# Second block of a two-block model: third sum read from PSUM, more products issued ahead with their results put aside, operands combined in place, another tail

## The chip, the core and the metric

The kernel runs on one core of one Trainium2 chip. The metric is device time in microseconds (us) of one execution. The kernel before was run three times: 2788.42 us in the median, 2787.32 to 2789.34. The engines of the core are called as the profile calls them: PE (matrix multiplications), PEld (its weight loads), DVE (vector), ACT (scalar), POOL (GpSimd), SP (the queue that issues almost all transfers of this part).

## The reference, cut to what matters

Two blocks are computed on a sequence of 1024 rows by 1024 features, in float32. Only the second one is touched here, of which only the last layer's end matters: a gated short convolution and a feed-forward part.

```
h = modulate(rmsnorm(x, norm1_g), sh1, sc1)          # 1024 x 1024
y = short_conv_mixer(h, conv_w_in, conv_w, conv_w_out)   # h @ (1024 x 3072), a gate and a
                                                     # 3-tap convolution, then @ (1024 x 1024)
x = x + g1 * y
h = modulate(rmsnorm(x, norm2_g), sh2, sc2)
gate, up = split(h @ ffn_w_in)                       # D_FF = 2816 columns each
x = x + g2 * ((silu(gate) * up) @ ffn_w_out)
return rmsnorm(x, final_g)
```

## The kernel before, in words

Each of the four big products is done in 2 x 2 blocks with seven block products instead of eight (P1 to P7, a Winograd scheme). Every float32 operand is split in a high and a low part, `split` (L106 the ACT cast that makes the high part, L107 the DVE subtraction that makes the low part), and each block product is three matmuls (high by high, high by low, low by high) for each of four blocks of 128 of the contraction: 12 matmuls of 128 x 512.

The stretch has four stages.

- **Conv, first product.** 12 sets (8 pairs of feature blocks, 4 gates), one set of 84 matmuls each. A set takes its left operands from the weights (`left_operands`: two loads of 512 KB through a ring of four raw buffers, then four sums on DVE, L1212 to L1216, and splits) and its right operands from the activations. These are seven slots in the pages H and HB, made by `right_operands` (four DVE operations L1177 to L1180 and `split_slots` L1167/L1169) for each of four blocks t of 128 rows. P1 and P2 need only right operands of the first 512 rows (B21, B11), all the others also some of the last 512 rows.
- **Conv, second product.** `out_products` (matmul L1335) runs over seven names in the order P1, P6, P2, P7, P5, P4, P3; `use` is called for each name and t with the result. `conv_use` closes the layer: the uses of P4 and P3 call `third`, which normalizes a row block, transposes it on PE (L1374) and makes the right operands of the feed-forward part.
- **Feed-forward, first product.** 22 sets as in the conv stage, `tail` L1241 to L1258 in each.
- **Feed-forward, second product.** `out_products` with `ffn_use`, whose P4 and P3 uses end with the final normalization (`fourth`, L1534) and the stores (L1535).

In a set, `head` does P1 and copies its result to an E tile (L1238). `tail` then does P6 (L1246 adds P1's copy), P5 (ACT copies the result from PSUM, L1248; POOL adds the sum so far, L1249: this is the third sum), P7 (L1251, DVE adds the third sum to the result), P2 (onto P1 in PSUM), P3 (L1255) and P4 (L1257). A set has four PSUM banks, and sets alternate between banks 0 to 3 and 4 to 7; P4 is accumulated onto P7's bank, so its first matmul comes after L1251. `ahead` L1260 does P1 and P2 of the first two sets of a stage before their other products.

Beside the sets POOL makes the second product's operands: `spill` combines what two sets gave (L1274 to L1280), and `sums_steps` combines blocks of the second weight (L1291 to L1307, their loads L1289 to L1306); both store to HBM. These steps are dealt out by `mix`, some at each tick.

The order on each engine is not that of the code: a scheduler sets it when the kernel is built, from the dependences and its own times of the instructions. SP and POOL are queues in that order as well.

Of the kernel before, what the change touches and what calls it, by code (L numbers as in the profile page):

```python
# [8 lines left out]
F32R = mybir.dt.float32r  # L9
AF = mybir.ActivationFunctionType  # L10
# [17 lines left out]
def program(tc, I, out):  # L28
# [4 lines left out]
    with ctx:  # L33
# [939 lines left out]
        def out_steps(half, i):  # L973
# [3 lines left out]
            def start():  # L977
                st["r"] = rr1()
# [139 lines left out]
        if 0:  # L1118
            with tc.manual_schedule(engines={mybir.EngineType.PE}):
                attention()  # L1120
        else:
            attention()
        for n in range(len((40, 43, 48, 52, 56, 59, 63)), 8):
            for x in out_steps(1, n):
                x()
# [9 lines left out]
        HBt = Split(sb(P3, "HB", 8192, F32R))  # L1135
        PA = Split(sb(P3, "PA", 2048, F32R))
        RAW.append(sb(P3, "raw3", 1024))
        E = sb(P3, "E", 18 * 512)
# [33 lines left out]
        def right_operands(where, t, h1, h2, tmp):  # L1172

            b11, b21, b12, b22 = h1[:, 0:512], h1[:, 512:1024], h2[:, 0:512], h2[:, 512:1024]
            t1, t2, t3, t4 = (tmp[:, i * 512:(i + 1) * 512] for i in range(4))
# [5 lines left out]
            split_slots(("T1", "T2"), where, t, tmp[:, 0:1024])  # L1181
            split_slots(("T3", "T4"), where, t, tmp[:, 1024:2048])


        n_set = {"i": 0}

        def left_operands(w, c1, c2):
# [3 lines left out]
            r1, r2 = next_raw(), next_raw()  # L1191
            SY.dma_start(r1.rearrange("p (k n) -> p k n", k=8), rows(w, c1, 128))
            SY.dma_start(r2.rearrange("p (k n) -> p k n", k=8), rows(w, c2, 128))
# [3 lines left out]
            def page():  # L1197
                w = wpages[turn["w"] % len(wpages)]
                turn["w"] += 1
                return w  # L1200
            g1, g2, g3 = page(), page(), page()
# [4 lines left out]
            def first():  # L1206
                split(g1.r[:, 0:1024], g1.r[:, 1024:2048], g1.f[:, 0:1024], r1)

            def rest():
                split(pa[:, 0:512], pa[:, 512:1024], paf[:, 0:512], r2[:, 0:512])  # L1210
# [3 lines left out]
                split(g2.r[:, 0:1024], g2.r[:, 1024:2048], g2.f[:, 0:1024], r2)  # L1214
                V.tensor_tensor(a12, a21, a12, ALU.subtract)
                V.tensor_tensor(a11, a11, a12, ALU.subtract)  # L1216
                split(g3.r[:, 0:1024], g3.r[:, 1024:2048], g3.f[:, 0:1024], r1)
            return dict(first=first, rest=rest, bank=4 * (i % 2), i=i,
                        w={"P1": half(g1, 512), "P2": half(g1, 0), "P5": half(g2, 0), "P7": half(g2, 512),
                           "P3": half(g3, 0), "P6": half(g3, 512),  # L1220
                           "P4": [pa[:, q * 512:(q + 1) * 512].rearrange("p (k n) -> p k n", k=4) for q in range(2)]})

        def product(st, name, where, start=True):
            ps = PS[:, st["bank"] + {"P1": 0, "P2": 0, "P6": 1, "P5": 2, "P3": 2, "P7": 3, "P4": 3}[name]]
# [8 lines left out]
        def head(st, where):  # L1233

            st["first"]()
            st["p1"] = U(st["i"] % 2)
            ps = product(st, "P1", where)
            A.copy(st["p1"], ps)  # L1238
            st["c11"] = ps

        def tail(st, where, c12):  # L1241

            st["rest"]()
            p1, p5 = st["p1"], U(2 + st["i"] % 2)
# [7 lines left out]
            if "early" not in st:  # L1252
                product(st, "P2", where, False)
# [4 lines left out]
            return st["c11"], c12, p1, p5  # L1258

        def ahead(sets, where):  # L1260
            for st in sets:
                head(st, where)
            for st in sets:
                product(st, "P2", where, False)
                st["early"] = True


        def spill(dst, j, even, odd, tmp):

            b11, b12, b21, b22 = even[:, 0:512], even[:, 512:1024], odd[:, 0:512], odd[:, 512:1024]  # L1270
            t1, t2, t3, t4 = (tmp[:, i * 512:(i + 1) * 512] for i in range(4))
# [9 lines left out]
            SY.dma_start(dst["T4"][j], t4)  # L1281

        def sums_steps(w, j, dst, a, b):
# [4 lines left out]
            def s1():  # L1288
                SY.dma_start(a, block(2, 2))  # L1289
                SY.dma_start(b, block(2, 1))  # L1290
                G.tensor_tensor(a, a, b, ALU.add)  # L1291
# [12 lines left out]

            def s3():
                SY.dma_start(a, block(1, 2))  # L1306
                G.tensor_tensor(a, a, b, ALU.subtract)  # L1307
                SY.dma_start(dst["S3"][j], a)
            return [s1, s2, s4, s3]

        def out_products(w, nj, right, sums, pages, use):
# [11 lines left out]
            for name in ("P1", "P6", "P2", "P7", "P5", "P4", "P3"):  # L1323
# [16 lines left out]
                last = js[-2:] if name == "P3" else []  # L1340
# [14 lines left out]
        N1 = {"B11": 1, "B21": 2, "B12": 0, "T1": 3, "T2": 4, "T3": 5, "T4": 6}  # L1355
        wpages = list(W)
# [3 lines left out]

        first = [left_operands(c_in, 1024 + f * 128, 2048 + f * 128) for f in range(2)]
        ahead(first, N1)

        xs = U(4, 2)
        SY.dma_start(xs, X2[7])
        tb = ring([5, 6, 7])
        for h in range(2):
# [256 lines left out]
```

## Time and profile before

| | |
|---|---|
| median of three runs | 2788.42 us (2787.32 to 2789.34) |
| the profiled execution's own time | 2781.8 us |
| its span in the trace | 2780.0 us |
| mean granted PE clock | 0.963 |
| PE, PEld, DVE, ACT, POOL busy in the span | 93%, 79%, 68%, 39%, 24% |

The stretch that is changed begins at about 1625 us. Its stages by the trace: the end of the first layer's last row block and the conv stage's preparation (to 1672.7), the conv products (to 1911.3), the conv's second product and the close of the layer (to 2074.1), the feed-forward's first product (to 2538.5), its second product (to 2747.9) and what follows the last matmul (to 2780.0). PEclk in the views is the clock that the throttle granted, 1.00 being the 2.4 GHz level and 0.50 the 1.2 GHz level; a mean between them is a stretch with both.

### The profile page before, as it was taken

What the parts mean: (1) busy time and instruction counts of PE and PEld (TensorE: products, weight loads), DVE (VectorE), ACT (ScalarE), POOL (GpSimd) and SP (SyncE); (2) the same over time, 40 slices, a digit from 0 to 9 for tenths busy, and PEclk for the clock granted to TensorE, in tenths of its full rate; (3) what the DMA queues carried; (4) which work ended last, traced back from release to release, by engine and by line L of the source; (5) the groups of instructions that cost most, each with busy time, mean ns of one, the idle gap of its engine ahead of it and who ended that gap; (6) DMA issues with size and microseconds to landing.
All of it is one profiled execution on the core that took longest, in us unless ns stands there. A gap on an engine that the chain in (4) does not pass through costs nothing.

```text
span 2780.0 us, 36848 instructions
## 1 busy us (share of the span) xinstructions
PE 2575.1 (93%) x13582; PEld 2206.0 (79%) x13582; DVE 1881.4 (68%) x3075; ACT 1080.5 (39%) x1911; POOL 675.0 (24%) x660
## 2 busy tenths in 40 slices
PE   8999999999999999999999958899649889999995
PEld 5799998879998878888898837787437767888884
DVE  5677776667778764656778957775686556776455
ACT  4332334323323543355657852223342223234332
POOL 2110000000003213133447732411223443212003
PEclk9999999999999999999999979999769999999997
DMA  7453343555444345432643244525555554326653
GB/s 256 144 148 111 95 133 115 159 180 152 123 126 152 114 137 178 171 107 61 221 143 115 81 142 142 161 87 170 170 174 189 185 191 144 103 96 216 201 189 137
DMA packets 326106, 411.73 MB, mean 148 GB/s; under 512 B 17622, under 2 KB 190190, under 8 KB 325410
## 3 DMA queue, kind: packets, MB, share of 16 engines
q1 hardware_dynamic: 318180, 398.36, 44.8%
q10 hardware_dynamic: 7744, 11.01, 1.1%
q8 instruction: 106, 1.74, 0.3%
q14 instruction: 76, 0.62, 0.1%
HBM read 315.40 MB, written 93.91 MB: 147 GB/s over the span
## 4 chain that ended last, share of the span: by engine, by line
PE 63%; DMA 16%; DVE 8%; POOL 5%; ACT 4%; issue 3%; SPq 1%; POOLq 0%; DVEq 0%; ACTq 0%
PE PS L516 15%; PE PS L1229 13%; PE PS L603 7%; PE PS L392 6%; PE PS L676 5%; DMA E<-in_ffn_w_out 4%; PE PS L1053 3%; PE PS L998 3%; PE PS L861 2%; PE PS L1335 2%; PE PS L895 2%; PE PS L883 2%; DMA raw<-SFS 2%; DVE H L107 2%; DMA E<-in_conv_w_out 2%
## 5 line engine op out<-in xcount | busy, mean ns | idle before, releaser
L1229 PE MATMUL PS<-H,w 128*128 128x512 f32 x1776 | 418.1, 393 | 22.4 <-ACT w L106 14.2
L1229 PEld LDWEIGHTS PS<-H,w 128*128 128x128 f32 x1776 | 336.7, 190 | 96.1 <-ACT w L106 15.4
L106 ACT CAST w<-raw 128x1024 fp32r<-128x1024 f32 x202 | 211.5, 1050 | 396.7 <-PE PS L1229 140.9
L107 DVE TENSOR_TENSOR w<-raw,w 128x1024 fp32r<-128x1024 f32 x200 | 266.7, 1338 | 117.2 <-ACT w L106 115.8
L516 PE MATMUL PS<-H,w 128*128 128x320 f32 x2112 | 320.5, 309 | 0.9 <-DVE TT L525 0.9
L516 PEld LDWEIGHTS PS<-H,w 128*128 128x128 f32 x2112 | 310.8, 188 | 3.0 <-DVE TT L525 1.2
L107 DVE TENSOR_TENSOR H<-raw,H 128x1024 fp32r<-128x1024 f32 (+1 forms) x133 | 166.4, 1262 | 123.0 <-ACT H L106 121.1
L1335 PE MATMUL PS<-H 128*128 128x512 f32 x924 | 216.0, 392 | 14.0 <-ACT H L106 13.9
L106 ACT CAST H<-raw 128x1024 fp32r<-128x1024 f32 (+1 forms) x133 | 134.1, 1018 | 233.0 <-DMA raw<-in_a_w_in 68.8
L1335 PEld LDWEIGHTS PS<-H 128*128 128x128 f32 x924 | 173.8, 189 | 52.7 <-ACT H L106 14.7
L339 POOL TENSOR_TENSOR H<-ACC,H 128x256 fp32r<-128x256 f32 x52 | 51.1, 983 | 609.7 <-ACT H L338 492.5
L1229 PE MATMUL PS<-HB,w 128*128 128x512 f32 x672 | 166.7, 401 | 16.7 <-ACT HB L1167 15.6
L1229 PEld LDWEIGHTS PS<-HB,w 128*128 128x128 f32 x672 | 128.0, 191 | 48.3 <-ACT HB L1167 16.0
L320 DVE SCALAR_TENSOR_TENSOR ACC<-raw,CO,ACC 128x512 f32<-128x512 f32 x182 | 133.8, 747 | 20.5 <-DMA raw<-in_ada_w 17.8
L516 PE MATMUL PS<-H 128*128 128x320 f32 x960 | 144.7, 309 | 0.0
L516 PEld LDWEIGHTS PS<-H 128*128 128x128 f32 x960 | 141.1, 188 | 0.5
L603 PE MATMUL PS<-w,H 128*128 128x512 f32 x600 | 140.0, 391 | 0.1
L1251 DVE TENSOR_TENSOR E<-PS,E 128x512 f32<-128x512 f32 x34 | 23.5, 691 | 162.9 <-POOL E L1249 121.9
L107 DVE TENSOR_TENSOR PTR<-PS,PTR 128x512 fp32r<-128x512 f32 x176 | 106.2, 613 | 36.5 <-ACT PTR L106 35.0
L603 PEld LDWEIGHTS PS<-w,H 128*128 128x128 f32 x600 | 111.5, 188 | 23.4 <-ACT TT L521 0.2
L392 PE MATMUL PS<-H 128*128 128x512 f32 x510 | 120.9, 391 | 0.0
L870 ACT ACTIVATE s<-s,sm 128x641 f32<-128x641 f32 (+1 forms) x128 | 103.3, 808 | 42.6 <-DVE sm L868 42.0
(329 smaller groups left out, 4971.7 us busy)
## 6 DMA issues: line engine op xcount, KB each, us to landing
raw<-in_a_w_in SPq DMA_DIRECT2D x96, 512.0 KB
raw<-in_ada_w SPq DMA_DIRECT2D x80, 512.0 KB
raw<-in_ffn_w_in SPq DMA_DIRECT2D x44, 512.0 KB
E<-in_ffn_w_out SPq DMA_DIRECT2D x66, 256.0 KB
raw<-in_a_w_out SPq DMA_DIRECT2D x32, 512.0 KB
raw<-in_conv_w_in SPq DMA_DIRECT2D x24, 512.0 KB
SFS<-E SPq DMA_DIRECT2D x44, 256.0 KB
TFT<-E SPq DMA_DIRECT2D x44, 256.0 KB
```

The costliest lines, as they stand in the source:

```text
L106: A.copy(hi, src)
L107: turn["split"] = (eng or V).tensor_tensor(lo, src, hif, ALU.subtract)
L320: V.scalar_tensor_tensor(ACC[:, s, :], r[:, j, :], CO[:, c, k:k + 1], ACC[:, s, :], ALU.mult, ALU.add)
L392: T.matmul(ps, HT[0][:, k, ap, t * 128:(t + 1) * 128], w[:, k % 2, :], start=k == 0 and n == 0, stop=k == 7 and n == 2)
L516: T.matmul(pss[h][:, 0:320], w[:, k, :], HT[0][:, k, ap, h * 320:(h + 1) * 320], start=k == 0 and n == 0, stop=k == 7 and n == 2)
L603: turn["mm"] = T.matmul(accs[t], ys[j].r[:, ap * 640 + t * 128:ap * 640 + (t + 1) * 128], wv[:, j, :], start=kp == 0 and j == 0 and n == 0 ...
L676: T.matmul(pss[j], HP[0][:, g + j, k, ap, :], w[:, k % 2, :], start=k == 0 and n == 0, stop=k == 7 and n == 2)
L870: A.activation(out=p[:, :nk + 1], in_=p[:, :nk + 1], func=AF.Exp, scale=-1.0, bias=sm[:, j:j + 1], accum_out=sm[:, 2 + j:3 + j])
L998: T.matmul(ps, o4[:, c, ap, :], w[:, c % 2, :], start=c == 0 and n == 0, stop=c == 3 and n == 2)
L1053: T.matmul(ps, w[:, k, :], HP[0][:, 2 + 4 * tg:6 + 4 * tg, k, ap, :], start=k == 0 and n == 0, stop=k == 7 and n == 2)
L1229: turn["mm"] = T.matmul(ps, w[:, k, :], b[:, ap, k, :], start=start and k == 0 and n == 0, stop=k == 3 and n == 2, skip_group_check=not start)
L1335: turn["mm"] = T.matmul(ps[:, t], x[ap][:, i, t * 128:(t + 1) * 128], s[v][:, i, :], start=new and j + i == 0 and q == 0, stop=j + i == nj ...
```

## The change

- The third sum is one DVE addition from PSUM in place of an ACT copy and a POOL addition.
- `ahead` does P1 and P2 of four sets (conv) and of six (feed-forward). Both results are copied to E tiles by ACT, so that the PSUM banks are free. Such a set loads its first weight block once for `first(False)`, and both blocks again in `rest`. In the feed-forward part the `first` of sets 0 to 3 is called in the use of P5, and the products in the use of P3.
- `right_operands` combines in place, two of its four operations on POOL for t < 3.
- E tiles are handed out by `Units`. The sums of the second weight start later (conv: after j = 1; feed-forward: after set 5), two j's interleaved.
- The last row block of the layer before stays in SBUF (`X7`) where it was stored and loaded again.
- Tail: P3's last four groups of operands are ordered t by t (two before). The use of P5 loads the second halves of the last 512 rows through the raw ring, adds them on POOL (L1601) and squares them into the raw buffer; the use of P4 loads the first halves.

```diff
-            A.copy(p5, c)
-            G.tensor_tensor(p5, p5, p1, ALU.add)
+            V.tensor_tensor(p5, c, p1, ALU.add)
...
-        def right_operands(where, t, h1, h2, tmp):
+        def right_operands(where, t, h1, h2, eng):
...
-            V.tensor_tensor(t1, b22, b21, ALU.subtract)
-            V.tensor_tensor(t2, b12, t1, ALU.subtract)
-            V.tensor_tensor(t3, b12, b22, ALU.subtract)
-            V.tensor_tensor(t4, b11, t2, ALU.subtract)
+            V.tensor_tensor(b21, b22, b21, ALU.subtract)
+            eng.tensor_tensor(b22, b12, b22, ALU.subtract)
+            V.tensor_tensor(b12, b12, b21, ALU.subtract)
+            eng.tensor_tensor(b11, b11, b12, ALU.subtract)
...
+            def first(keep=True):
+                r = load(c1)
+                if keep:
+                    st["r"] = r, load(c2)
...
             def rest():
+                r1, r2 = st["r"] if "r" in st else (load(c1), load(c2))
...
+        def ahead(st, where, bank, p1, c11):
+            ps = product(st, "P1", where, ps=PS[:, bank])
+            A.copy(U(p1), ps)
+            product(st, "P2", where, False, ps=ps)
+            A.copy(U(c11), ps)
+            st.update(p1=p1, c11=c11)
...
-                last = js[-2:] if name == "P3" else []
+                last = js[-4:] if name == "P3" else []
...
             elif name == "P5":
                 V.tensor_tensor(u3, ps, u3, ALU.add)
                 G.tensor_tensor(u3, u3, gbs[1], ALU.mult)
+                first[t]["first"](False)
...
                 third(4 + t, xs, u2)
+                if t == 0:
+                    ahead(first[0], N3, 0, 8, 9)
+                else:
+                    ahead(first[t], N3, t, *((10, 11) if t == 1 else (t - 2, t + 2)))
+                if t >= 2:
+                    first[t + 2]["first"](False)
+                    ahead(first[t + 2], N3, t - 2, t, t + 4)
...
             elif name == "P5":
                 V.tensor_tensor(u3, ps, u3, ALU.add)
                 G.tensor_tensor(u3, u3, gbs[1], ALU.mult)
+                x = next_raw()[:, 0:512]
+                SY.dma_start(x, X3[4 + t][:, 512:1024])
+                G.tensor_tensor(u3, u3, x, ALU.add)
+                mean_square(MS[:, 4 + t, 1:2], u3, x)
...
-                fourth(t, xs)
-                if t == 3:
-                    for q in range(4):
-                        x, u = late[q], U(q)
-                        SY.dma_start(x, X3[4 + q])
-                        G.tensor_tensor(x[:, 512:1024], x[:, 512:1024], U(4 + q), ALU.add)
...
+                fourth(t, [xs[:, 0:512], xs[:, 512:1024]])
+                SY.dma_start(r, X3[4 + t][:, 0:512])
+                G.tensor_tensor(u2, u2, gbs[0], ALU.mult)
+                G.tensor_tensor(r, r, u2, ALU.add)
```

PE at the end of the conv's second product, before (L1335 its matmuls, L1374 the transposes of `third`, L1229 the set products of the feed-forward part):

```order
L1335 MATMUL PS<-HB 128x512 x6
L1374 MATMUL PS<-ident,raw_181 128x128 x4
L1374 MATMUL PS<-ident,raw_13955 128x128 x4
L1374 MATMUL PS<-ident,raw_181 128x128 x4
L1374 MATMUL PS<-ident,raw_13955 128x128 x4
L1374 MATMUL PS<-ident,raw_183 128x128 x8
L1374 MATMUL PS<-ident,raw_182 128x128 x8
L1229 MATMUL PS<-H,w_177 128x512 x2
```

The same place of the change (L1376, L1404 and L1254 are the same three in its numbering):

```order
L1376 MATMUL PS<-HB 128x512 x6
L1254 MATMUL PS<-H,w_178 128x512 x12
L1254 MATMUL PS<-H,w_179 128x512 x2
L1404 MATMUL PS<-ident,raw_181 128x128 x4
L1254 MATMUL PS<-H,w_179 128x512 x8
L1404 MATMUL PS<-ident,raw_183 128x128 x4
L1254 MATMUL PS<-H,w_179 128x512 x2
L1254 MATMUL PS<-H,w_180 128x512 x4
L1254 MATMUL PS<-HB,w_178 128x512 x12
L1254 MATMUL PS<-H,w_180 128x512 x3
L1404 MATMUL PS<-ident,raw_181 128x128 x4
```

The set products, which stood behind the last transpose, now stand between the transposes: 96 of them ahead of the fifth group of four transposes, 144 in all.

ACT in the feed-forward's second product, before, from P5's last operands to P4's (L106 casts operands for PE; the squares L922 of the output stood behind the last of these, sixteen in a row):

```order
L106 CAST H<-raw_183 128x512
L106 CAST H<-raw_182 128x512
L106 CAST H<-raw_181 128x1024
L106 CAST H<-raw_182 128x1024
L106 CAST H<-raw_181 128x1024
```

The same place of the change:

```order
L106 CAST H<-raw_13954 128x512
L106 CAST H<-raw_182 128x512
L922 ACTIVATE raw_181,MS<-E 128x512
L922 ACTIVATE raw_182,MS<-E 128x512
L922 ACTIVATE raw_13954,MS<-E 128x512
L922 ACTIVATE raw_181,MS<-E 128x512
L106 CAST H<-raw_182 128x1024
L106 CAST H<-raw_13954 128x1024
```

Four squares now stand in ACT's order between P5's last casts and P4's first, and the three raw buffers they write are those that P4's operands are loaded into next.

## Rows read from the trace of the kernel before

**Rows 1.** Busy time by stage; start:end, us, each engine (instructions), clock, DMA.

```profile
1624.70:1672.70 48.00, 16.06 (x65) 12.34 (x64) 34.00 (x63) 23.39 (x44) 8.69 (x7) 0.69 0.49 153
1672.70:1775.00 102.30, 90.36 (x368) 71.89 (x369) 69.21 (x83) 23.56 (x30) 36.69 (x25) 0.93 0.50 157
1775.00:1911.30 136.30, 136.30 (x595) 111.81 (x594) 102.95 (x118) 37.89 (x45) 24.96 (x16) 1.00 0.33 105
1979.60:2074.10 94.50, 30.98 (x115) 20.64 (x114) 69.36 (x124) 45.46 (x96) 26.00 (x20) 0.60 0.59 200
2074.10:2340.00 265.90, 241.21 (x984) 194.16 (x985) 155.78 (x194) 71.80 (x96) 98.69 (x70) 0.94 0.57 183
2340.00:2530.00 190.00, 190.00 (x830) 155.46 (x829) 139.92 (x157) 61.83 (x83) 44.95 (x30) 1.00 0.34 113
2538.50:2747.90 209.40, 209.40 (x923) 172.91 (x921) 108.73 (x114) 76.47 (x90) 23.71 (x18) 1.00 0.59 195
2747.90:2780.00 32.10, 0.23 (x1) 0.00 (x0) 19.80 (x35) 7.78 (x22) 15.97 (x15) 0.56 0.42 148
```

**Rows 2.** PE's waits in the feed-forward sets: us in total, times, longest us.

```profile
PE PS L1229 <- DVE E L1251: 24.7, 7, 5.6
```

**Rows 3.** PE's waits in the conv sets, 1672.7 to 1911.3, same columns.

```profile
PE PS L1229 <- DVE E L1251: 10.4, 4, 7.8
```

**Rows 4.** Groups by line from 1615 us on: busy us, mean ns, idle before, releasers.

```profile
L107 DVE TENSOR_TENSOR w<-raw,w 128x1024 fp32r<-128x1024 f32 x102 | 133.5, 1316 | 32.6 <-ACT w L106 31.3
L1249 POOL TENSOR_TENSOR E<-E 128x512 f32<-128x512 f32 x34 | 46.2, 1358 | 191.8 <-ACT E L1248 185.3 <-DVE E L1246 6.5
L1251 DVE TENSOR_TENSOR E<-PS,E 128x512 f32<-128x512 f32 x34 | 23.5, 691 | 162.9 <-POOL E L1249 121.9 <-PE PS L1229 40.9
L1248 ACT COPY E<-PS 128x512 f32<-128x512 f32 x34 | 19.9, 586 | 128.1 <-PE PS L1229 128.1
```

**Rows 5.** PE's timeline into the feed-forward sets: start, us, operation, idle before.

```profile
2027.20 0.60 PE L1374 MATMUL PS<-ident,raw 128*128 128x128 f32 x4
...
2052.92 1.11 PE L1374 MATMUL PS<-ident,raw 128*128 128x128 f32 x4 [7.23 <-ACT raw L1379]
...
2070.78 1.22 PE L1229 MATMUL PS<-H,w 128*128 128x512 f32 x2 [12.10 <-ACT w L106]
2074.14 11.69 PE L1229 MATMUL PS<-H,w 128*128 128x512 f32 x39 [2.13 <-ACT w L106]
```

**Rows 6.** SP's timeline, the last reload of activations before the feed-forward sets.

```profile
2062.38 0.53 SPq L1455 DMA_DIRECT2D raw<-HR  x1
```

**Rows 7.** DVE's timeline at the last right operands of the feed-forward part.

```profile
2071.25 1.76 DVE L1213 TENSOR_TENSOR raw<-raw,raw 128x512 f32<-128x512 f32 x1
...
2079.83 0.68 DVE L1169 TENSOR_TENSOR H<-E,H 128x512 fp32r<-128x512 f32 x1
```

**Rows 8.** POOL's timeline there, two additions of one size.

```profile
2034.39 1.27 POOL L1291 TENSOR_TENSOR E<-E 128x512 f32<-128x512 f32 x1
...
2039.25 4.72 POOL L1296 TENSOR_TENSOR E<-E 128x512 f32<-128x512 f32 x1 [1.83 <-DMA E<-in_ffn_w_out]
```

**Rows 9.** DVE's timeline, the last right operand of the conv stage.

```profile
1678.11 0.69 DVE L1169 TENSOR_TENSOR HB<-E,HB 128x512 fp32r<-128x512 f32 x1
```

**Rows 10.** SP's timeline at the end: P4's first operands, stores, reloads, last stores.

```profile
2662.24 1.15 SPq L121 DMA_DIRECT2D raw<-TFT  x2
...
2735.61 2.47 SPq L1535 DMA_DIRECT2D out<-E  x4
2739.39 1.56 SPq L1552 DMA_DIRECT2D E<-X  x2
...
2770.95 5.16 SPq L1535 DMA_DIRECT2D out<-E  x8
```

**Rows 11.** DVE's timeline at the end, the last outputs.

```profile
2773.02 2.73 DVE L1534 SCALAR_TENSOR_TENSOR E<-E,RX,raw 128x512 f32<-128x512 f32 x4
```

**Rows 12.** PE's timeline, the last matmuls.

```profile
2747.28 0.85 PE L1335 MATMUL PS<-H 128*128 128x512 f32 x3
```

More of the change, by code (lines that the diff above doesn't have):

```diff
@@ L977, in start @@
             def start():
-                st["r"] = rr1()
+                st["r"] = X7 if half and i == 7 else rr1()
                 if half:
@@ L1213, in rest, with product @@
                 V.tensor_tensor(a22, a12, a22, ALU.subtract)
-                split(g2.r[:, 0:1024], g2.r[:, 1024:2048], g2.f[:, 0:1024], r2)
+                p = page()
+                split(p.r[:, 0:1024], p.r[:, 1024:2048], p.f[:, 0:1024], r2)
                 V.tensor_tensor(a12, a21, a12, ALU.subtract)
                 V.tensor_tensor(a11, a11, a12, ALU.subtract)
[L1217 to L1224, printed above, removed]
+                q = page()
+                split(q.r[:, 0:1024], q.r[:, 1024:2048], q.f[:, 0:1024], r1)
+                st["w"].update(P5=half(p, 0), P7=half(p, 512), P3=half(q, 0), P6=half(q, 512),
+                               P4=[pa[:, j * 512:(j + 1) * 512].rearrange("p (k n) -> p k n", k=4) for j in range(2)])
+                st["rest"] = lambda: None
+            st.update(first=first, rest=rest)
+            return st
+        def product(st, name, where, start=True, ps=None):
+            if ps is None:
+                ps = PS[:, st["bank"] + {"P1": 0, "P2": 0, "P6": 1, "P5": 2, "P3": 2, "P7": 3, "P4": 3}[name]]
             b = slot_views(where[RIGHT[name]])[0][:, 0]
@@ L1231, in product, with seven @@
             return ps
[L1233 to L1241, printed above, removed]
+        def ahead(st, where, bank, p1, c11):
[4 more added lines that the diff above has]
+            st.update(p1=p1, c11=c11)
+        def seven(st, where, units, c12):
+            early = "c11" in st
+            if not early:
+                st["first"]()
+                st["p1"] = units.get()
+                c11 = product(st, "P1", where)
+                A.copy(U(st["p1"]), c11)
+            else:
+                c11 = U(st["c11"])
             st["rest"]()
-            p1, p5 = st["p1"], U(2 + st["i"] % 2)
+            held = [st["p1"], units.get()] + ([st["c11"]] if early else [])
+            p1, p5 = U(held[0]), U(held[1])
             b = product(st, "P6", where)
@@ L1257, in tail, with spill @@
             V.tensor_tensor(p1, d, p1, ALU.add)
[L1258 to L1271, printed above, removed]
+            return c11, p1, p5, held
+        def spill(dst, j, even, odd, units):
+            (b11, b12), (b21, b22) = even, odd
+            ids = [units.get() for _ in range(4)]
+            t1, t2, t3, t4 = (U(i) for i in ids)
             for name, x in (("B11", b11), ("B21", b21), ("B12", b12)):
@@ L1359, in program @@
         f_in, f_out = I["ffn_w_in"][0], I["ffn_w_out"][0]
[L1361 to L1367, printed above, removed]
-            mean_square(MS[:, 0, h:h + 1], xs[:, h * 512:(h + 1) * 512], U(8 + h))
-        rms(RM[:, 0:1], MS[:, 0, :])
-        V.tensor_scalar(xs, xs, RM[:, 0:1], None, op0=ALU.mult)
         def feature_blocks(src, dst, half, scol, bcol, ps):
@@ L1435, in program @@
         xsr = ring([U(12, 2), U(14, 2)])
+        n_set["i"] = 0
+        first = [left_operands(f_in, f * 128, (NFF + f) * 128) for f in range(6)]
         def third(i, xs, junk):
@@ new lines, in program @@
+            c12 = units.get()
+            c11, c21, c22, held = seven(st, N3, units, U(c12))
+            y = []
+            for x1, x2 in ((c11, c21), (U(c12), c22)):
+                y.append(units.get())
+                s1 = U(y[-1])
+                A.activation(out=s1, in_=x1, func=AF.Tanh, scale=0.5)
+                V.scalar_tensor_tensor(s1, s1, 1.0, x1, ALU.add, ALU.mult)
+                V.scalar_tensor_tensor(s1, s1, 0.5, x2, ALU.mult, ALU.mult)
+            units.put(c12, *held)
@@ L1514, in program @@
             ys.append(y)
             if f % 2:
-                spill(TF, f // 2, ys[0], ys[1], U(12, 4))
+                spill(TF, f // 2, *((U(a), U(b)) for a, b in ys), units)
+                units.put(*ys[0], *ys[1])
                 ys = []
+            if f == 5:
+                mix.begin(sums(f_out, NFF // 2, SF, [units.get() for _ in range(4)]), NFF - 7)
             mix.tick()
```

161 lines of the change are left out of this document (87 added, 74 removed).

## The prediction, made before the changed kernel ran

> **What bounds the kernel now.** I read the busy time by stage first, then PE's waits, then the timelines at the edges of the stages. The chain of waits is a sum over the whole program, so I read the stages instead.
>
> In the steady part of both sets' stages PE is busy all the time at the full 2.4 GHz level: 190.00 us for 830 matmuls in the feed-forward sets, .229 us each; the conv sets 136.30 for 595, the same [rows 1]. So a set of 84 costs 19.2 us there, DVE is second with 139.92 of 190.00 (14.1 us a set), and ACT and POOL are far off. Nothing that only frees ACT, POOL or DVE gains in these stretches.
>
> PE is not the bound in three places. First, the preparations: 16.06 us busy of 48.00 before the conv sets and 30.98 of 94.50 before the feed-forward sets, there at a granted clock of 0.60 [rows 1]. Secondly, the first part of both stages of sets, where PE waits for L1251, in all 10.4 us (conv) and 24.7 (feed-forward) [rows 2, 3]; L1251 in turn waited 121.9 of its 162.9 us for POOL's third sum [rows 4], since POOL there also makes the second product's sums (98.69 us busy in 265.90, against 44.95 in 190.00 later [rows 1]). Thirdly, the 32.1 us behind the last matmul [rows 1].
>
> The sums are made against the profiled execution's own 2781.8 us, a span of 2780.0. The median of 2788.4 is 6.6 above it; I add that back at the end.
>
> **Feed-forward sets (the large term).** Before, they run from 2074.1 to 2538.5, 464.4 us, for 22 x 84 = 1848 matmuls, 423 us at .229. The loss of 41 is the 24.7 us of waits plus matmuls at the lower clock after each and at the start (39 in 11.69 us, .30 each [rows 5]).
>
> The third sum from PSUM takes 34 copies of .586 us off ACT, 34 additions of 1.36 off POOL, and puts 34 of about .69 (L1251's own duration, the same form) on DVE [rows 4]. With POOL out of the chain, what is late next is DVE: it has 5 us to spare in a set of 19.2. I take the L1251 waits as gone.
>
> The early products: P1 and P2 are 24 matmuls, for six sets 144. They move into the gap, so 1704 remain, 390.2 us. These sets are 60 matmuls long, 13.7 us. DVE's work per set falls by one split (1.3 us [rows 4]) and rises by .69, from 14.1 to 13.5, so DVE and PE are level. I allow 5 us of stalls for the six.
>
> When do they start? The last right operand was made at 2080.5 [rows 7], behind a reload of activations issued only at 2062.38 [rows 6] and transposes that go on after 2052.92 [rows 5]. In the change's order on PE, 96 early products stand before the fifth group of transposes. At the lower clock (four transposes take 1.11 us at 2052.92, against .60 at 2027.20 [rows 5]) they would be some 40 us of work; from 2027 on PE was nearly idle for 43 us in before [rows 5]. They fill that idle time, and I let the last split stay at 2080.5. Two POOL operations in the last chains cost 4 more. P6, first now, waits for the set's left sums and split, some 3.5 us, which P1 and P2 used to cover: 2088. End: 2088 + 390 + 5 = 2483 against 2538.5: **-55**. Bounds: -68 (start at 2080, no stalls, a faster clock in the gap) and -20 (early products push the transposes back by their whole 40 us at the low clock, less the waits still removed).
>
> The first splits of sets 0 to 3, now in P5's use, are four DVE splits of 1.3 us and four loads of 512 KB, beside PE's work between the conv sets and the gap (1911.3 to 1979.6 [rows 1]); I take +1 (0 to +3), for a late operand.
>
> A place to weigh is POOL's share of the right operands. POOL's addition at 2039.25 took 4.72 us, against 1.27 for the same operation at 2034.39 [rows 8]; a DVE addition at 2071.25 took 1.76, against .68 for a similar one [rows 7]. By rows, the six moved operations save DVE 4.1 us and put at most two POOL operations of 1.3 to 4.7 on the last chain: the 4 us above.
> The Trainium skill (SBUF — State Buffer, "SBUF: two separate sides") says that DVE with two SBUF inputs and GpSimd share one port pair as an exclusive lock, held for the whole instruction, so that the other "fully blocks"; the two long rows agree with it. By that rule nothing is gained by the move, since the time comes back as blocking, and the sum would be 4 us worse, -51.
>
> **Conv sets.** Before: 1672.7 to 1911.3, 238.6 us, for 960 matmuls (the P1 and P2 of two sets already lay in the gap), 219.8 at .229; 18.8 lost, 10.4 of it waits for L1251 [rows 3]. After: 912 remain, 208.8. DVE was busy 34.0 of 48.0 in the preparation [rows 1] and made its last right operand at 1678.8 [rows 9]; six operations fewer (-4) and two first splits more (+2.6), a shorter way to the last rows (X7 stays in SBUF), P6's operands as above: start near 1680. Stalls 6: four short sets whose DVE work is 102.95/136.30 x 19.2 = 14.5 us, -1.3 + .7 = 13.9 against 13.7, and early results in the same PSUM banks as the first sets. End 1895: **-16**. Bounds: -28 (start 1674, no stall) and +2 (P6 waits for all right operands, which come at 1690, and the sums, started after j = 1, press on the second half).
>
> **Feed-forward's second product and tail.** Two terms of opposite sign. P4's first operands were loaded at 2662.24 [rows 10], long before P5's end near 2688 (2538.5 and five sevenths of 209.40 [rows 1]). In the change, ACT has four squares before P4's casts, and P4's loads want the raw buffers that the squares write. The squares wait for P5's last results: P5's first t is done 2 us before its end, and from there run a DVE addition (.7), eight POOL operations of 1.27 [rows 8] in a row (10.2), a square (.8), two casts (2 x 1.05) and a DVE split (1.3). PE stands still for 13 to 14 us, runs at the lower clock behind it (+2, as after 2074.14 [rows 5]), and P3's end waits 2 more for its bundled operands: **+17**, bounds +5 and +22.
>
> Behind the last matmul (2748.1 [rows 12]) 32.1 us pass. The path is SP's: stores issued at 2735.61 release the buffers for reloads at 2739.39, and so on to the last stores at 2770.95 [rows 10]. With P3's last four groups ordered t by t, 7 operand pairs in a row for each t, the first t ends 63 matmuls, 14.3 us, before the last, against 27 matmuls, 6.1 us; operands are done 8 us earlier relative to the end, and half the reloads are gone from the chain. What must stay behind the last matmul is two additions, a square, the norm, two scalings, the stores: about 10 us, of which 4.2 from the last scaling (2773.02 + 2.73 [rows 11]) to the end. Taking the chain's other buffers into account I put it at 16: **-16** (-20 to -8). Net +1, bounds -14 to +14.
>
> **Sum.** -55 + 1 - 16 + 1 = -69: 2713 in the profiled execution, **2719 us** on the scale of the median. The outer bounds together are -110 and -1.
>
> **The rivals.**
> A. The early products displace the transposes. For it: PE has the 96 products ahead of the fifth group in its order, and at 0.60 of the clock; against it: 43 us of idle time stand there. The feed-forward gain is then 25 instead of 55: **2749**.
> B. The gap ends earlier than I think. The reload at 2062.38 [rows 6] stood behind stores of the sums, which the change starts only after set 5. If the chain of the last rows is shorter by 16 us, and the tail gains 12 more: **2691**. Against it: DVE's work (69.36 of 94.50 [rows 1]) doesn't shrink.
> C. Slower: the raw ring of four paces the early sets. Each of the ten wants both blocks loaded again in 13.7 us, through buffers that the set before releases only after its last split. A set that lasts longer than 20.6 us (13.7 + 69/10) costs more than all the gain; at 22 us it is 10 x 8.3 = 83 lost: **2802**. For it: each of the 102 splits has an ACT cast before it, and sets took 22.7 us in 2074 to 2340 (265.90 x 84/984 [rows 1]); against it: those were paced by the third sum [rows 2], and steady sets do the same loads in 19.2.
> D. DVE paces the early sets, as it is level with PE and its operations are longer beside POOL's [rows 7]. At 18 us for a set 10 x 4.5 = 45 are lost: **2764**, still faster.
>
> **How the numbers follow.** Forecast .58, A .15, B .13, C .07, D .07. No change means within 0.2%, 5.6 us, which is what a measurement can tell. Forecast, A and B are faster throughout; of D a small part ends within or above it: faster .91, same .02, slower .07. The forecast's own range is 2698 to 2743 (conv and feed-forward 10 us either way, the tail 14). The range for 8 in 10 reaches into A and B, not to C: 2688 to 2757.
>
> **What would show it.** Right: the waits for L1251 are gone from PE's table; the feed-forward sets start near 2088 and end near 2483 on before's scale, their first six at 13.7 to 14.5 us; PE stands still for about 13 us between P5 and P4 with POOL's addition and the square as its releasers; 16 us remain behind the last matmul. Wrong: transposes of the last rows ending after 2080 (A) or a feed-forward start before 2075 (B); casts in the early sets waiting for DMA (C); PE waiting for DVE splits there (D).

## The result, and the profile after

The changed kernel takes 2760.1 us in the median of four runs (2756.9 to 2765.8), before 2788.9 on the same chip: a ratio of 0.9896 (95% interval 0.9875 to 0.9918), 29 us faster. The prediction was faster, but by 69, and the time lies above its range. The profiled execution took 2762.0 us, its span is 2760.2, 19.8 less than before's; the rest of the 29 is the place of the two profiled executions among their runs (before's took 2781.8, 7 us less than its median). Ratios, here and below, are of executions in the usual, fast state alone; a single execution of experiment 6 lasted 8325 us and is not in its ratio.

The busy time by stage of the changed kernel, columns as in [rows 1]:

```profile
1680.40:1775.00 94.60, 88.72 (x382) 70.99 (x382) 71.77 (x94) 18.26 (x21) 7.01 (x4) 1.00 0.28 85
...
1968.00:2085.50 117.50, 68.48 (x264) 49.84 (x262) 76.10 (x130) 56.33 (x115) 22.00 (x20) 0.74 0.43 143
2085.50:2170.00 84.50, 76.96 (x303) 60.62 (x304) 63.76 (x77) 19.95 (x25) 15.43 (x9) 0.92 0.41 129
2170.00:2340.00 170.00, 160.60 (x695) 129.58 (x693) 133.62 (x144) 43.46 (x56) 86.30 (x55) 0.99 0.73 237
2340.00:2509.00 169.00, 164.78 (x711) 134.62 (x712) 126.60 (x143) 49.31 (x64) 32.95 (x21) 0.98 0.42 136
...
2658.50:2735.80 77.30, 63.23 (x264) 51.54 (x264) 40.94 (x45) 29.77 (x42) 18.52 (x17) 0.89 0.60 187
2735.80:2760.20 24.40, 0.04 (x1) 0.00 (x0) 19.41 (x34) 5.05 (x14) 9.39 (x10) 0.59 0.42 151
```

The gap before the feed-forward sets (the second row shown; in before the fourth of [rows 1]) is longer, 117.5 against 94.5 us, and full of early products: 68.48 us of PE against 30.98, at a granted clock of 0.74 against 0.60. The sets from 2085.5 to 2340 still don't fill PE. Behind them a new hole stands in 2658.5 to 2735.8 (63.23 of 77.30).

PE's waits in the feed-forward sets (2085.5 to 2530), columns as in [rows 2]. The waits for the addition after P7 are gone (24.7 us at L1251; in the change it is L1284, which no row names), and PE waits 1.8 us for the third sum itself, now L1282. Others stand in their place: for ACT's casts of left operands (L106; 10.9 of the 15.8 is the wait at the start, where before waited 12.10 [rows 5]) and for ACT's copy of P1 (L1273):

```profile
PE PS L1254 <- ACT w L106: 15.8, 5, 10.9
PE PS L1254 <- ACT E L1273: 13.2, 3, 11.6
PE PS L1254 <- DVE E L1282: 1.8, 3, 1.4
PE PS L1254 <- DVE w L107: 1.3, 1, 1.3
```

PE's timeline at the places where it lost time, columns as in [rows 5]: the start of the sets, three of the short waits among the early ones, the copy's wait, the bubble between P5 and P4 of the second product, the last matmuls:

```profile
2085.50 19.42 PE L1254 MATMUL PS<-H,w 128*128 128x512 f32 x72 [10.89 <-ACT w L106]
...
2118.59 7.57 PE L1254 MATMUL PS<-H,w 128*128 128x512 f32 x32 [1.40 <-ACT w L106]
2127.17 1.20 PE L1254 MATMUL PS<-H,w 128*128 128x512 f32 x4 [1.01 <-ACT w L106]
2129.63 7.06 PE L1254 MATMUL PS<-H,w 128*128 128x512 f32 x24 [1.26 <-DVE w L107]
...
2344.22 7.35 PE L1254 MATMUL PS<-HB,w 128*128 128x512 f32 x24 [11.60 <-ACT E L1273]
...
2672.57 14.01 PE L1376 MATMUL PS<-H 128*128 128x512 f32 x48 [14.08 <-ACT H L106]
...
2734.99 0.85 PE L1376 MATMUL PS<-H 128*128 128x512 f32 x3
```

The stages from such timelines, each as a length, so that a shift of one does not count in the next (each from one execution; the conv sets' end, in nine kernels with the same conv code, lies between 1896.8 and 1907.5, so a few us in one stage of one trace mean little):

| | before | predicted | after |
|---|---|---|---|
| end of the conv sets | 1911.5 | -16 | 1899.0, -12.5 |
| from there to the end of P3 (conv's second product) | 115.9 | +1 | 119.3, +3.4 |
| from there to the end of the feed-forward sets | 511.1 | -55 | 490.8, -20.3 |
| feed-forward's second product | 209.7 | +17 | 226.7, +17.0 |
| from the last matmul to the end | 31.9 | -16 | 24.4, -7.5 |
| sum | | -69 | -19.9 |

Of the 49 us that are missing by the two traces, 35 are in the feed-forward sets.

### The profile page after: what moved, and what is told of

Read it like the earlier page. It is cut to its first block, busy times and chain, and to the rows that moved or that the text cites. A ratio compares the mean times of both kernels' runs of the same rounds, so it can differ in the third digit from the quotient of the medians.

```text
span 2760.2 us, 36848 instructions
## 1 busy us (share of the span) xinstructions
PE 2575.8 (93%) x13582; PEld 2202.0 (80%) x13582; DVE 1922.2 (70%) x3097; ACT 1067.2 (39%) x1887; POOL 652.1 (24%) x638
## 4 chain that ended last, share of the span: by engine, by line
PE 71%; DVE 10%; DMA 9%; ACT 4%; issue 3%; POOL 3%; SPq 0%; DVEq 0%; POOLq 0%; ACTq 0%
PE PS L516 16%; PE PS L1254 14%; PE PS L1376 8%; PE PS L603 7%; PE PS L676 5%; PE PS L392 5%; PE PS L1053 3%; PE PS L998 2%; PE PS L861 2%; PE PS L895 2%; PE PS L883 2%; DVE w L107 1%; PE PS L497 1%; DMA E<-in_ffn_w_out 1%; DMA raw<-in_a_w_in 1%
## 5 line engine op out<-in xcount | busy, mean ns | idle before, releaser
L1254 PE MATMUL PS<-H,w 128*128 128x512 f32 x1776 | 432.5, 400 | 42.5 <-ACT w L106 21.7
L1254 PEld LDWEIGHTS PS<-H,w 128*128 128x128 f32 x1776 | 340.9, 193 | 123.8 <-ACT w L106 25.9
L106 ACT CAST w<-raw 128x1024 fp32r<-128x1024 f32 x202 | 211.1, 1050 | 509.5 <-PE PS L1254 134.4
L1376 PE MATMUL PS<-H 128*128 128x512 f32 x924 | 220.1, 397 | 29.7 <-ACT H L106 29.7
L1376 PEld LDWEIGHTS PS<-H 128*128 128x128 f32 x924 | 176.9, 192 | 69.6 <-ACT H L106 30.9
L106 ACT CAST H<-raw 128x1024 fp32r<-128x1024 f32 (+1 forms) x133 | 134.1, 1018 | 212.0 <-DMA raw<-in_a_w_in 71.3
L1254 PE MATMUL PS<-HB,w 128*128 128x512 f32 x672 | 169.5, 404 | 23.0 <-ACT E L1273 13.2
L1254 PEld LDWEIGHTS PS<-HB,w 128*128 128x128 f32 x672 | 127.0, 191 | 58.6 <-ACT E L1273 14.4
L106 ACT CAST PTR<-PS 128x512 fp32r<-128x512 f32 x176 | 91.8, 524 | 54.4 <-PE PS L883 49.8
```

The source lines that it names most:

```text
L106: A.copy(hi, src)
L1254: turn["mm"] = T.matmul(ps, w[:, k, :], b[:, ap, k, :], start=start and k == 0 and n == 0, stop=k == 3 and n == 2, skip_group_check=not start)
L1376: turn["mm"] = T.matmul(ps[:, t], x[ap][:, i, t * 128:(t + 1) * 128], s[v][:, i, :], start=new and j + i == 0 and q == 0, stop=j + i == nj ...
```

## The experiments

All are timed in rounds beside the kernel before; ratios are to before on the same chip (before's medians 2785 to 2788).

**1. The third sum alone, in the kernel before; and the old third sum in the changed kernel.**

The edit of the kernel before; the second run undoes the same edit in the changed kernel.

```diff
-            A.copy(p5, c)
-            G.tensor_tensor(p5, p5, p1, ALU.add)
+            V.tensor_tensor(p5, c, p1, ALU.add)
```

> The kernel before with the third sum from PSUM alone. By the prediction's step (the waits for L1251 go and no others come): the 35 us of waits and the slower matmuls after them, 40 to 50 us faster than before, 2740 to 2749. Rival (what POOL and the second product's sums held up is late elsewhere, for E tiles that POOL frees late, or DVE): 10 to 25 us faster.

Measured: 0.9893 (0.9880 to 0.9906), 30 us faster than before; the edit alone gives as much as the whole change. Neither number fits: it lies between. In its trace PE waits no longer for the addition after P7 (L1250 there), but for the third sum itself (L1248), 15.9 us in the feed-forward sets where before lost 24.7 at L1251:

```profile
PE PS L1229 <- DVE E L1248: 15.9, 5, 6.7
```

The longest of these waits ends at 2268.58, when the third sum has run. It stood on DVE behind left sums that take 1.63 us and not .68:

```profile
2265.49 1.63 DVE L1216 TENSOR_TENSOR raw<-raw 128x512 f32<-128x512 f32 x1
2267.83 0.69 DVE L1248 TENSOR_TENSOR E<-PS,E 128x512 f32<-128x512 f32 x1
```

> The changed kernel with the old third sum (ACT copy, POOL addition). By the prediction's step: the waits of L1251 come back wherever POOL makes the second product's sums, 25 to 40 us slower than the changed kernel. Rival (with the sums later and the early sets shorter, POOL is free when it counts): less than 12 us slower.

Measured: 2766.7, 0.9928 (0.9912 to 0.9943), 9 us slower than the changed kernel by the ratios (the intervals overlap a little). The rival's number is right. 19.7 us of waits for the addition after P7 are back (L1285 there), while other waits are shorter: the first 360 matmuls of the sets, as many as the six early sets have, take 89.4 us in this trace and 98.9 in the changed kernel. So the third sum brings 30 us alone and 9 beside the other parts. That it is the later sums of the second weight which make up the difference, as the rival has it, was not tested: they never ran alone.

**2. The tail's loads in free E tiles.**

```diff
-                x = next_raw()[:, 0:512]
+                x = U(12 + t)
```

> The changed kernel, with one line changed: in the feed-forward part the second halves that P5's use loads go to free E tiles (12 + t) and not through the raw ring. Theory (the bubble is the raw ring and ACT's order: P4's operands wait for the squares): PE's 14 us between P5 and P4 and the slow matmuls behind it go, 15 to 18 us less than the changed kernel, 2742 to 2745. Rival (the squares stand ahead of P4's casts in ACT's order whatever buffer they write): the bubble stays, within 3 us of the changed kernel.

Measured: 2748.8, 0.9870 (0.9856 to 0.9884), 7 us faster than the changed kernel by the ratios (the two intervals overlap a little); by the trace 17: the second product takes 209.5 us as in before, and P4 follows P5 without a pause (the last 60 matmuls of P5 and the first 48 of P4, which stood apart at 2672.57, in one row):

```profile
2643.63 24.68 PE L1376 MATMUL PS<-H 128*128 128x512 f32 x108
```

So the loads through the raw ring made the bubble. The run does not separate the ring from ACT's order, which changed with it: the four squares now stand behind the casts of P4's first operands, so that the rival's premise no longer held. What follows the last matmul grew from 24.4 to 26.7: part of the time saved is waited away there.

**3. Two and four early sets in the feed-forward part.** The calls for the sets left out go too, and the E tiles that these sets would hold are free from the start; here for four.

```diff
-        first = [left_operands(f_in, f * 128, (NFF + f) * 128) for f in range(6)]
+        first = [left_operands(f_in, f * 128, (NFF + f) * 128) for f in range(4)]
-                if t >= 2:
-                    first[t + 2]["first"](False)
-                    ahead(first[t + 2], N3, t - 2, t, t + 4)
-        units = Units(12, 13, 14, 15, 16, 17)
+        units = Units(12, 13, 14, 15, 16, 17, 2, 6, 3, 7)
```

> The changed kernel with two early sets in the feed-forward part and not six. By the prediction's step (an early set saves its 24 matmuls, 5.5 us): 22 us slower than the changed kernel. Theory now (early sets are paced by their second load of the weights through the raw ring, they took about 16.3 us each and not 13.7): 4 x 2.9 = 10 to 13 us slower. Rival (the gap and the first sets hang on the right operands alone and the early sets give nothing): within 4 us.

Measured: 2748.2, 0.9873 (0.9858 to 0.9888). All three numbers were wrong, the first two in sign: two early sets are faster than six, by 6 us by the ratios (these intervals overlap), 14.4 by the spans. Experiment 6 shows the same difference clear of noise.

> The changed kernel with four early sets in the feed-forward part and not six. Theory (sets 4 and 5, loaded between the last two row blocks' buffers, push the right operands and the first set back by the whole 19 us that stand between two and six early sets): start near 2067 to 2070, and 11 us more of matmuls: 5 to 8 us faster than the changed kernel, the best of two, four and six. Rival (each early set pushes the start by the same amount, 4.8 us): start near 2076, within 3 us of the changed kernel's half way to two early sets, about 4 faster.

Measured: 2754.0, 0.9883 (0.9864 to 0.9902), between two and six and not apart from either. The start, 2071.6 where P3 ended 4.3 us later than in the change, was as the theory has it; the gain was not there. The last transposes and first products of the sets, in the change, with two and with four early sets:

```profile
2067.48 0.60 PE L1404 MATMUL PS<-ident,raw 128*128 128x128 f32 x4
```

```profile
2053.53 1.12 PE L1404 MATMUL PS<-ident,raw 128*128 128x128 f32 x4 [4.73 <-ACT raw L1409]
2066.49 3.78 PE L1254 MATMUL PS<-H,w 128*128 128x512 f32 x8 [11.84 <-ACT w L106]
```

```profile
2057.75 1.11 PE L1404 MATMUL PS<-ident,raw 128*128 128x128 f32 x4 [2.14 <-ACT raw L1409]
2071.64 2.08 PE L1254 MATMUL PS<-H,w 128*128 128x512 f32 x4 [12.78 <-ACT w L106]
```

Counted from P3's end (2018.3, 2015.8, 2022.6) the last transposes come at 49, 38 and 35 us, the sets' start at 67, 51 and 49. So in these traces, one each, sets 3 and 4 cost the preparation nothing, and sets 5 and 6, whose loads stand between the buffers of the last two row blocks, 16 to 18 us. From the start to the end of the sets, though, it is 423.6 (six), 429.1 (four) and 427.2 us (two), for 1704, 1752 and 1800 matmuls: what early sets spare PE comes back as waits and as matmuls at the lower clock.

**4. Another order of the raw ring, once.** Before the feed-forward sets the ring is turned so that set 0's second load takes the buffer of set 5's first block.

```diff
+        n = turn["raw"] % 4
+        order = RAW[n:] + RAW[:n]
+        RAW[:] = [order[0], order[3], order[1], order[2]]
+        turn["raw"] = 0
```

> The changed kernel (six early sets) with the raw ring's order changed once, before the feed-forward sets: set 0's second load takes the buffer of set 5's first block and not one that the last right operands hold. Theory (the late start is in part that second load, which waits for DVE's last right-operand split at 2078): the products after the gap start 5 to 8 us earlier than 2085.5 and the kernel is 4 to 8 us faster than the changed one. Rival (the start hangs on the right operands themselves, late because set 4's and 5's loads take turns in the ring): start within 2 us, time within 3.

Measured: 2752.7, 0.9877 (0.9858 to 0.9895), 5 us faster by the ratios (the intervals overlap). The start came at 2076.0 and not 2085.5, with three matmuls still before it:

```profile
2073.44 1.06 PE L1254 MATMUL PS<-H,w 128*128 128x512 f32 x3 [1.97 <-ACT w L106]
2076.04 10.28 PE L1254 MATMUL PS<-H,w 128*128 128x512 f32 x33 [1.54 <-ACT w L106]
```

The theory holds for the start: 9.5 of the 16 to 18 us were this load.

**5. All four operations of the right operands on DVE**, in both stages.

```diff
-            right_operands(N1, t, a, b, G if t < 3 else V)
+            right_operands(N1, t, a, b, V)
```

> The changed kernel with all four operations of the right operands on DVE in both stages. By the prediction's step (two POOL operations cost 4 us on the last chain): 2 to 5 us faster than the changed kernel. Rival (DVE is what the preparation waits for, and POOL's operations run beside it): 2 to 5 us slower.

Measured: 2755.8, 0.9887 (0.9870 to 0.9904): 2 us faster, not apart from the changed kernel. So neither the theory nor the rival is shown.

**6. Two early sets and the tail in E tiles together.**

> Two early sets in the feed-forward part and the tail's loads in free E tiles, both edits together. Theory (the two losses lie in different stages and add): 15 us faster than either alone by the trace, near 2734 on this scale (2785 for before). Rival (the tail's end is set by SP's stores and reloads, so that an earlier last matmul is waited away): 5 us faster than either alone.

Measured: 2740.2, 0.9831 (0.9815 to 0.9847), 11 to 12 us faster by the ratios than with either edit alone: between the two numbers, nearer to the first, and with intervals that stand apart from both. The losses lie in different stages and nearly add. Behind the last matmul now stand 30.1 us.

**7. On top of that: the sums earlier, the same with experiment 5's edit, the sums on two tiles, two early sets in the conv stage.**

```diff
-            if f == 5:
-                mix.begin(sums(..., [units.get() for _ in range(4)]), NFF - 7)
+            if f == 1:
+                mix.begin(sums(..., [units.get() for _ in range(4)]), NFF - 3)
```

> Two early sets, tail in free E tiles, and the second product's sums begun after set 1 over 19 ticks and not after set 5 over 15. Theory (the wait of 7 to 12 us near set 10, ACT's copy of P1 for a tile that a store still reads, comes from POOL's queue, which stands behind the sums' crowded loads): the wait is gone or under 3 us, 5 to 8 us faster than without this edit, a ratio to before near 0.981. Rival (tiles are short as such): the wait stays or comes earlier, within 3 us.

Measured: 0.9835 (0.9821 to 0.9848), no gain. The wait for the copy went, as the theory has it, and PE's waits in the sets are down to little more than these; but the time is the same. A wait of 4.3 us for the third sum came up among the first sets, and the sets started 1.7 us later behind P3 than in experiment 6:

```profile
PE PS L1254 <- ACT w L106: 10.8, 1, 10.8
PE PS L1254 <- DVE E L1282: 5.1, 2, 4.3
```

> The same and all four operations of the right operands on DVE. Theory (POOL's two operations lengthen the chains of both preparations by 3 to 5 us): the conv sets end some 4 us earlier and the feed-forward sets start earlier by as much again, ratio near 0.979. Rival (what one run of it alone gave, 2 us, was the spread of runs): the same as without, 0.981.

Measured: 0.9853 (0.9839 to 0.9867), if anything slower. The conv sets ended 4.1 us earlier, at 1895.8, as in experiment 5 (1894.2; 1896.8 to 1907.5 in the nine kernels with two operations on POOL). So the theory's step is there in both traces. It did not come through: the feed-forward sets took 6.1 us more, with a wait of 7.3 for ACT's copy of P1, and the second product 4.6. Whether the edit brought these is not shown. In time neither run gained beyond its interval, which is what the rival, spread, says.

```diff
-                mix.begin(sums(..., [units.get() for _ in range(4)]), NFF - 7)
+                sb2 = [units.get() for _ in range(2)]
+                mix.begin([x for q in range(NFF // 2) for x in sums_steps(..., U(sb2[0]), U(sb2[1]))], NFF - 7)
```

> Two early sets, tail in free E tiles, and the sums one block pair at a time with two E tiles and not two at a time with four, begun after set 5 as in the change. Theory (the wait near set 10 is POOL standing behind loads): POOL then waits for each load in turn, the wait stays or grows, 0 to 8 us slower than without this edit. Rival (tiles are short): two more tiles free the copy, the wait goes, 5 to 8 us faster.

Measured: 0.9879 (0.9866 to 0.9893), 13 us slower than without. Neither number fits: the wait for the copy went, as the rival has it, but PE waits for the third sum instead (17.1 us), and POOL for loads of the sums 166 us in all against 87 in experiment 6 and 94 in the changed kernel. So freeing two tiles is not what helps here; that POOL's waits for loads make the third sum late is argued from these two numbers and not shown.

```profile
PE PS L1254 <- DVE E L1282: 17.1, 7, 4.3
```

```diff
-        first = [left_operands(c_in, 1024 + f * 128, 2048 + f * 128) for f in range(4)]
+        first = [left_operands(c_in, 1024 + f * 128, 2048 + f * 128) for f in range(2)]
```

> Two early sets, tail in free E tiles, and two early sets in the conv stage too, not four. By the prediction's step (an early set saves 5 us): 8 to 11 us slower than without this edit. Theory now (early sets give back what they save, as in the feed-forward stage): within 4 us.

Measured: 2735.9, 0.9822 (0.9809 to 0.9835): the same as four early sets in the conv stage (0.9831 in experiment 6; the intervals overlap). The prediction's step is wrong there too.

**8. Less of DVE's work in the six early sets.** The kernel leaves out the product with the up projection in these sets, so its result is another.

```diff
-                V.scalar_tensor_tensor(s1, s1, 0.5, x2, ALU.mult, ALU.mult)
+                if f >= 6:
+                    V.scalar_tensor_tensor(s1, s1, 0.5, x2, ALU.mult, ALU.mult)
```

> The changed kernel (six early sets) without the last DVE operation of each half in the first six feed-forward sets: it leaves out the product with the up projection there, 12 operations of .7 to 1.8 us. Theory (DVE paces the early sets, 17.8 us busy of 19 in one stretch, with PE waiting for casts that wait for DVE's sums): the six sets, 100 us in the changed kernel, take 8 to 14 us less. Rival (the second load through the raw ring paces them): within 3 us of 100.

Measured: 2748.8, 0.9865 (0.9846 to 0.9884), 9 us faster than the changed kernel by the ratios (the intervals overlap a little); the first 360 matmuls of the sets took 92.8 us and not 98.9. Between the two numbers, nearer to DVE: 12 operations of about .8 us, 9.6 in all, gave 6 back in these sets. Experiment 1's second run, where DVE lacks the third sum, points the same way (89.4).

**9. Two early sets in both stages and the sums begun after set 1, together.**

> Third sum and tail of the change with the tail's loads in free E tiles, two early sets in both stages, sums begun after set 1: the edits of three earlier runs together. Theory (each of them gives 0 to 3 us): ratio to before 0.981 to 0.983, the best of all so far or level with it. Rival (the sums begun early cost the first sets what they free later): 0.9835 or more.

Measured: 2741.0, 0.9838 (0.9820 to 0.9856). No better than its parts. The lowest ratio of all is 0.9822, the change with the tail's loads in E tiles and two early sets in both stages; experiments 6, 7 (sums begun after set 1) and 9 are not apart from it.

## Why the prediction was wrong, by its own steps

**The early feed-forward sets** are the step that failed: "These sets are 60 matmuls long, 13.7 us ... I allow 5 us of stalls for the six", and a start at 2088. Measured against P3's end the start is 6.6 us later than forecast, the six sets (the first 360 matmuls) take 98.9 us and not 87, and the sixteen later ones 325 and not 308.

- The start. I named rival A (early products push the transposes back) and rival C (the raw ring) and priced the forecast without them. Both are in it, though neither as I wrote it. The last transposes end 50 us behind P3 and not 31, which is 2077 on before's scale and short of my sign for A (2080); and the ring delays the start, while inside the early sets no cast waits for a load. Experiment 3 shows 16 to 18 us that sets 5 and 6 cost before the start, experiment 4 that half of them is a load waiting for a buffer. The right operands, now combined in place, hold that buffer until DVE's last split at 2078. My 43 us of idle PE were there, but the early products took raw buffers, not only PE time.
- The six sets. "DVE and PE are level" was too simple. Over these sets DVE is busy 71 of 97 us, but where the spill's POOL operations run beside it, its sums take 1.7 us and not .69, and there it is busy nearly all the time (17.79 of 19.00). Columns as in [rows 1], then DVE's timeline in the changed kernel and POOL's beside it:

```profile
2116.00:2135.00 19.00, 15.32 (x59) 11.61 (x59) 17.79 (x19) 4.85 (x6) 7.05 (x4) 0.91 0.57 177
2088.00:2185.00 97.00, 88.73 (x360) 69.90 (x359) 70.98 (x87) 21.89 (x28) 18.90 (x12) 0.95 0.43 139
```

```profile
2122.56 1.78 DVE L1233 TENSOR_TENSOR raw<-raw 128x512 f32<-128x512 f32 x1
2124.37 1.67 DVE L1234 TENSOR_TENSOR raw<-raw,raw 128x512 f32<-128x512 f32 x1
2126.07 1.64 DVE L1237 TENSOR_TENSOR raw<-raw,raw 128x512 f32<-128x512 f32 x1
2127.75 0.69 DVE L1238 TENSOR_TENSOR raw<-raw 128x512 f32<-128x512 f32 x1
```

```profile
2121.57 2.21 POOL L1301 TENSOR_TENSOR E<-E 128x512 f32<-128x512 f32 x1 [0.63 <-DVE E L1559]
2123.86 1.62 POOL L1303 TENSOR_TENSOR E<-E 128x512 f32<-128x512 f32 x1
2125.56 1.60 POOL L1307 TENSOR_TENSOR E<-E 128x512 f32<-128x512 f32 x1
```

  PE then waits 1 to 1.4 us for ACT's cast, which waits for these sums (ACT's waits in 2088 to 2185):

```profile
ACT w L106 <- DVE raw L1234: 19.7, 4, 7.5
```

  This is rival D in kind, at 16.5 us a set where D has 18. Of the 16.5 us that 360 matmuls take beyond .229 each, the waits behind the start are 8.3; the rest is slower matmuls. The clock falls after some of the waits and not after others: from 2118.59 on 32 matmuls run in 7.57 us at a granted clock of 1.00, from 2129.63 on 24 in 7.06 at 0.80. Experiment 8 shows 6 of the 11.5 us above the forecast as DVE's; what paces the rest was not settled.
- The later sets. This loss I did not have at all. With the sums of 11 block pairs in 15 ticks, POOL stands behind a load, the spill behind POOL, its store behind the spill, and ACT's copy of P1 behind the store, whose tile it wants. POOL (L1339 and L1326 of the sums, L1305 and L1301 of the spill), the spill's store and ACT in the changed kernel:

```profile
2334.28 1.73 POOL L1339 TENSOR_TENSOR E<-E 128x512 f32<-128x512 f32 x1 [7.57 <-DMA E<-in_ffn_w_out]
2335.97 1.71 POOL L1305 TENSOR_TENSOR E<-E 128x512 f32<-128x512 f32 x1
2337.64 1.71 POOL L1326 TENSOR_TENSOR E<-E 128x512 f32<-128x512 f32 x1
2339.31 1.71 POOL L1301 TENSOR_TENSOR E<-E 128x512 f32<-128x512 f32 x1
```

```profile
2341.04 0.32 SPq L1302 DMA_DIRECT2D TFT<-E  x1
```

```profile
2343.59 0.59 ACT L1273 COPY E<-PS 128x512 f32<-128x512 f32 x1 [9.42 <-DMA TFT<-E]
```

  PE waits 11.6 us for that copy. With the third sum from PSUM and the sums begun after set 5 on four tiles, such a wait stands in every trace, 6 to 12 us long; begun after set 1 it was gone in one of three traces, 2.0 us in another (experiments 7 and 9) and 7.3 in the third, and the time no shorter.

**The conv sets**: -12.5 for -16, near by luck and not for the reason given. The third sum alone brings 8.6 of it (one trace each), and two early sets do as well as four.

**The third sum**: the waits for L1251 went as forecast, but "what is late next is DVE" was given no price, and alone the edit left 15.9 us of waits for the third sum on DVE. Alone it is worth the whole gain of the change; beside the other parts about 9 us.

**The bubble** was right in place and size: 14.08 us for 13 to 14 predicted, with the releasers named. That the stage comes out at +17.0 for +17 is in part luck: the 48 matmuls behind the bubble took 14.01 us, 3 above .229 each and not 2, and the 2 us of P3's end were not there (PE has no other wait after 2600). POOL and ACT, whose last square is followed by P4's first cast, here held by its load:

```profile
2657.26 3.73 POOL L1598 TENSOR_TENSOR E<-E 128x512 f32<-128x512 f32 x3 [43.94 <-DVE E L1597]
...
2663.40 3.70 POOL L1601 TENSOR_TENSOR E<-E,raw 128x512 f32<-128x512 f32 x3
```

```profile
2667.13 0.63 ACT L922 ACTIVATE raw<-E 128x512 f32<-128x512 f32 x1 [0.50 <-POOL E L1601]
...
2669.15 1.04 ACT L106 CAST H<-raw 128x1024 fp32r<-128x1024 f32 x1 [1.29 <-DMA raw<-TFT]
```

**The tail** was a mis-sized term: -7.5 for -16. I named SP's chain of stores and reloads as the path and then let it shrink with the matmuls. It stays: reloads of first halves are issued after the last matmul (2735.8), behind stores:

```profile
2731.65 0.33 SPq L1605 DMA_DIRECT2D E<-X  x1
2738.82 0.33 SPq L1613 DMA_DIRECT2D E<-X  x1
...
2745.84 0.43 SPq L1613 DMA_DIRECT2D E<-X  x1
2746.32 11.31 SPq L1584 DMA_DIRECT2D out<-E  x9
```

Without the bubble it is 26.7 and 30.1 us (experiments 2 and 6) for before's 31.9, so the new tail by itself gives 2 to 5. What its parts give was not tested one by one.

**The range** assumed that the terms would not all miss on one side. Four of five did. In the large one the work was counted at PE's rate, and the buffers and engines that feed it were given 5 us. One slip in the sums: rival D's ten sets at 18 us and not 13.7 lose 43 us, not 45.

## What to carry to other kernels

Work that is moved into a gap of the bound engine takes that gap's buffers along: count for each moved step whose buffer its loads take in the ring, and who holds that buffer last. A set made shorter for PE is only as short as the second engine lets it be, and that engine is to be counted at its slow rate where a neighbour shares its time. Test the parts of a large change alone: here one line gave as much as all of it, and undoing others gave 18 to 21 us more.

## What the runs showed of the hardware that was not expected

DVE additions with both inputs in SBUF and POOL additions of the same size, back to back on both engines, take 1.6 to 1.8 us each (2122 to 2128 above), one of each every 1.7 us, against .69 and 1.27 alone. The prediction's rule (the Trainium skill, SBUF — State Buffer, "SBUF: two separate sides": an exclusive lock for the whole instruction) would by an estimate make a pair last .69 + 1.27 = 1.96 (1.84 by the spacing of such additions alone: .60 on DVE, in before from 2068.23 on, and 1.24 on POOL, at 2657.26 above); the pairs here last 1.7, so in this case the engines do not exclude each other for all of both instructions. That they hold each other up is as the page has it, and here it costs DVE most: 1.0 us for each operation, POOL .3 to .5.
